# A two-layer trunk on one core: another order in the mixer and the last head, and a third tile's products ahead of the first down products of each SwiGLU

## The chip, the cores and the metric

The kernel runs on one core of one Trainium2 chip. The metric is the device time of one execution in microseconds (us). Engines are named as in the profile: PE is TensorE, DVE VectorE, ACT ScalarE, POOL GpSimd, SP the engine that issues most loads.

## The reference

What must be computed, cut to the two layers (T = 1024 frames, D = 1024 features, float32 in and out):

```python
def conv_pool_mixer(h, w_in, dw_w, dw_b, ln_g, ln_b, pool_w, pool_scale, w_out):
    z = h @ w_in
    a = a_val * jax.nn.sigmoid(a_gate)
    a = depthwise_causal_conv(a, dw_w, width=31) + dw_b
    a = jax.nn.silu(layernorm(a, ln_g, ln_b))
    d = trailing_mean(u, window=2/4/8/16 per group) - u
    p = einsum('btgc,gcd->btgd', d, pool_w) * pool_scale
    return jnp.concatenate([a, p], axis=-1) @ w_out
def hgrn2_mixer(h, w_in, lb, gn_g, w_out):
    q, f_raw, i, g = jnp.split(h @ w_in, 4, axis=-1)
    f = lb + (1 - lb) * sigmoid(f_raw); k = 1 - f
    o = chunkwise_recurrence(q, k, i, f)
    o = head_rmsnorm(o) * gn_g * jax.nn.silu(g)
    return o @ w_out
def swiglu_ffn(h, w1, w3, w2):
    return (jax.nn.silu(h @ w1) * (h @ w3)) @ w2
```

Layer 0 adds the mixer of the normalized h to h, then the SwiGLU of the normalized h; layer 1 does so with HGRN; a last RMSNorm follows.

## The kernel before

Frames lie along the free axis of a tile, features along the partitions. The 1024 frames are two halves of 512 (`half`); a tile is 128 features by 512 frames, and 8 of them (`KT`) make a half of the residual. The residual lives in HBM, in `hd[k]`. A step either adds to it by an accumulating DMA from POOL's queue (`accumulate`, L304), or fetches it, adds a PE bank to it on DVE (`add_residual`, L328) and puts it back. `Ahead` (L315) fetches three tiles before they are needed.

Each float32 product is made of three matmuls of a rounded high part and a low rest (`gemm_steps`, L154): high by high, high by low, low by high, 512 columns each. So each operand is split, high part on ACT, low part on DVE (`split` L170 for activations, `load` L135 for weights: SP fetches 128x1024 float32 into one of two raw buffers, ACT and DVE write a pair out of three). PE banks come from two pools of four (`gbank`, `mbank`).

The order on each engine is fixed when the program is built: a scheduler takes the instructions by priority, which is the order of the code unless a block raises it (`tc.high_priority`, `sooner`). Each engine and each DMA queue then works its list in order, waiting at the head of the list.

**Mixer** (`layer0_mixer`, L335). x is transposed on PE, normalized and split; `project_a` makes the gated conv input of four channel tiles; `conv` (L464) runs the 31 taps of channel tiles 0, 1 and 2 on DVE in steps of 512 columns; tile 3 goes through PE (`conv_by_phase`, L512) with weights that `conv_blocks` builds on POOL from the taps (L506), and its result is regrouped by small DMAs into `cb` and brought into y3 by four activations (L539). The pooling groups follow (`project_u`, `map_u`, `mean_u`: banks u, uw and um; the tile v between them, L583, is made by ACT). Then the projection of the pooled half (banks op, 16 of them, 12 products each), with ACT copying each bank out and POOL adding it to the residual; the layer norm of the conv half (L621 on: ysum, mu, lss, the broadcast bc_ln), both halves of the frames one after the other; and the conv half's projection (banks oa), which fetches the residual, adds and puts back. All of the pooling steps and the op products stand in one block of raised priority, the layer norm in one of still higher priority.

**SwiGLU** (`ffn`, L668). 22 hidden tiles in blocks of 2, 4, 4, 4, 4, 4 (`BLOCKS`, L664). A tile's two products over all 1024 frames are seven products of half the depth (`Up.p1` to `p7`, 12 matmuls each) with sums of weights (`sums`) and sums of inputs (b11, b21, b22, t1 to t4); `gate` applies the norm's row and the SiLU. The first pair of tiles goes step by step together (p1, p2, p6, p7, p4, then gate(0), p5, p3, gate(1)). Behind each block come its down products (banks f0o and f1o); for the first block these are 16 banks of 6 products.

**HGRN** (`hgrn`, L883). 8 heads. `recur` (L974) runs one head's recurrence for one half; at each of its steps it yields a number (`BEFORE`, L911) of filler products which the caller pulls in front of the step (`advance`). The filler of a head is the projection of the next head (pf, pq, the values pv, and pg, the output gate) and, where `OUT_AT` (L912) says so, products of the output projection (banks ho) of heads that are done. What is left of the filler follows at the head's end. The output projection of the filler is accumulated; for that ACT copies the bank into one of three buffers (`temp`). The last two steps behind head 7 fetch the residual, add and put back (h_ho).

```python
BEFORE = {0: 7, 2: 4, 4: 5, 6: 3, "k": 2, "S": 2, "o": 1, "T": 10}
OUT_AT = {3: (([0, 1], (0, 1)),), 7: (([2, 3], (0, 1)), ([4, 5], (0,)))}
```

## Time and profile before

| | us |
|---|---|
| median of 3 runs (lowest, highest) | 2321.64 (2317.51, 2322.33) |
| profiled execution, its own time | 2319.05 |
| its span in the profile | 2317.2 |
| PE busy | 2233.5 (96%) |
| DVE busy | 1566.5 (68%) |
| ACT busy | 836.7 (36%) |
| POOL busy | 330.1 (14%) |

The mean granted clock of PE over the span is 0.983 of full speed. The mixer runs from the start to about 325 us, the first SwiGLU to about 1000, HGRN to about 1625, the second SwiGLU and the last norm to the end. The profile's rows are of one execution; a wait's time is put down to the event that came last. In the stretches below, the first figure behind the length is PE's busy time, so length minus that is its idle time.

### The profile page before, as it was taken

The numbers are of one execution on the slowest core, as the hardware profiler recorded it, in microseconds if no ns is written. First come the engines' busy times: TensorE is split into PE (matmuls) and PEld (weight loads), VectorE is DVE, ScalarE is ACT, GpSimd is POOL, SyncE is SP. The second block draws the span as 40 slices with busy tenths as digits, with TensorE's granted clock in tenths as the row PEclk, the third lists the DMA queues.
The fourth block names the chain that finished last, engine by engine and source line by source line (L and its number), as shares of the span: only waits on it lengthen the run. The fifth ranks groups of instructions, "written<-read, shape, count | busy, mean of one in ns | idle before, by whom it ended". The sixth has DMA issues, their size and how long they took to land.

```text
span 2317.2 us, 28669 instructions
## 1 busy us (share of the span) xinstructions
PE 2233.5 (96%) x10814; PEld 1873.9 (81%) x10814; DVE 1566.5 (68%) x2924; ACT 836.7 (36%) x1354; POOL 330.1 (14%) x341
## 2 busy tenths in 40 slices
PE   7998999999999999999999899988899999999998
PEld 6887777888888888888888789876688888888877
DVE  6999695738373736858887387866956464737377
ACT  5223654333333333532222322234543333323336
POOL 1030334010101010310000200035220101010110
PEclk9998999999999999999999999998999999999999
DMA  7103735161515252631111611176153434242544
GB/s 230 56 11 80 186 116 109 55 127 55 117 54 113 62 111 71 210 100 37 46 46 37 118 37 47 37 140 188 55 109 91 91 86 96 74 99 73 100 136 155
DMA packets 220746, 218.18 MB, mean 94 GB/s; under 512 B 9332, under 2 KB 181568, under 8 KB 220608
## 3 DMA queue, kind: packets, MB, share of 16 engines
q1 hardware_dynamic: 186320, 130.18, 18.5%
q0 software_dynamic: 27008, 73.41, 17.1%
q10 hardware_dynamic: 7280, 12.76, 1.5%
q8 instruction: 85, 1.39, 0.2%
q14 instruction: 53, 0.43, 0.1%
HBM read 137.67 MB, written 77.59 MB: 93 GB/s over the span
## 4 chain that ended last, share of the span: by engine, by line
PE 56%; issue 25%; DVE 9%; POOL 2%; DMA 2%; ACT 1%; SPq 0%; ACTq 0%; POOLq 0%; DVEq 0%
PE f1o L160 3%; PE f1o L161 3%; PE f1o L162 3%; PE f0o L161 3%; PE f0o L162 3%; PE f0o L160 3%; DVE y L470 3%; POOL hd L308 1%; DVE wl L143 1%; PE op L160 1%; PE op L161 1%; PE op L162 1%; PE f_5p L735 1%; PE f_18p L735 1%; PE f_18p L733 1%
## 5 line engine op out<-in xcount | busy, mean ns | idle before, releaser
L143 DVE TENSOR_TENSOR wl<-wr,wh 128x1024 fp32r<-128x1024 f32 x130 | 161.4, 1241 | 108.4 <-ACT wh L142 107.7
L142 ACT CAST wh<-wr 128x1024 fp32r<-128x1024 f32 x132 | 138.5, 1051 | 147.1 <-PE pg L161 19.3
L470 DVE SCALAR_TENSOR_TENSOR y<-a,dww,y 128x512 f32<-128x512 f32 x180 | 137.1, 810 | 0.4
L308 POOL DMA_DIRECT2D hd<-ev_ho x40 | 34.8, 892 | 542.0 <-ACT ev_ho L307 534.4
L1029 DVE COPY_PREDICATED S<-masks,pl 128x128 f32<-128x128 uint8 x288 | 92.2, 341 | 13.2 <-PE pl L1011 12.0
L160 PE MATMUL f1o<-f1g_1h,wh 128*128 128x512 f32 (+1 forms) x208 | 74.6, 359 | 1.9 <-ACT f1ev L858 1.9
L1011 PE MATMUL pl<-M,K 128*128 128x192 f32 x384 | 73.0, 334 | 3.5 <-DVE M L998 3.5
L161 PE MATMUL f1o<-f1g_1l,wh 128*128 128x512 f32 (+1 forms) x208 | 74.1, 356 | 0.0
L162 PE MATMUL f1o<-f1g_1h,wl 128*128 128x512 f32 (+1 forms) x208 | 74.1, 356 | 0.0
L160 PE MATMUL f1o<-f1g_0h,wh 128*128 128x512 f32 x176 | 69.3, 393 | 4.2 <-DVE f_0u L762 2.9
L160 PE MATMUL f0o<-f0g_0h,wh 128*128 128x512 f32 x176 | 69.2, 393 | 2.4 <-DVE f_0u L762 2.4
L1011 PEld LDWEIGHTS pl<-M,K 128*128 128x128 f32 x384 | 65.5, 194 | 6.9 <-ACT M L1001 2.2
L161 PE MATMUL f1o<-f1g_0l,wh 128*128 128x512 f32 x176 | 69.5, 395 | 1.1 <-DVE f1g_0l L174 1.1
L160 PE MATMUL f0o<-f0g_1h,wh 128*128 128x512 f32 x176 | 68.6, 390 | 1.4 <-ACT f0ev L858 1.4
L162 PE MATMUL f1o<-f1g_0h,wl 128*128 128x512 f32 x176 | 69.1, 392 | 0.4 <-DVE wl L143 0.4
L162 PE MATMUL f0o<-f0g_0h,wl 128*128 128x512 f32 x176 | 69.2, 393 | 0.0
L161 PE MATMUL f0o<-f0g_0l,wh 128*128 128x512 f32 x176 | 69.1, 393 | 0.0
L161 PE MATMUL f0o<-f0g_1l,wh 128*128 128x512 f32 x176 | 68.6, 390 | 0.1
L162 PE MATMUL f0o<-f0g_1h,wl 128*128 128x512 f32 x176 | 68.5, 389 | 0.0
L864 ACT COPY f1ev<-f1o 128x512 f32<-128x512 f32 x64 | 37.4, 585 | 80.1 <-PE f1o L162 66.1
L864 ACT COPY f0ev<-f0o 128x512 f32<-128x512 f32 x64 | 37.4, 585 | 78.7 <-PE f0o L162 67.2
L866 POOL DMA_DIRECT2D hd<-f0ev x32 | 27.8, 869 | 219.6 <-ACT f0ev L864 217.3
(5437 smaller groups left out, 7075.6 us busy)
## 6 DMA issues: line engine op xcount, KB each, us to landing
wr<-in_ffn_w SPq DMA_DIRECT2D x56, 512.0 KB, 3.4
...
hd<-ev_ho POOLq DMA_DIRECT2D x40, 256.0 KB, 5.2
h_f<-hd POOLq DMA_DIRECT2D x32, 256.0 KB, 5.4
...
```

Of the source, the lines that this page charges most:

```text
L142: nc.scalar.copy(wh, raw)
L143: (leng or nc.vector).tensor_tensor(wl, raw, f32(wh), ALU.subtract)
L160: nc.tensor.matmul(ps, lh, xh, start=k == 0, stop=False)
L161: nc.tensor.matmul(ps, lh, xl, start=False, stop=False)
L162: mm = nc.tensor.matmul(ps, ll, xh, start=False, stop=k == len(xs) - 1)
L308: nc.gpsimd.dma_start(out=hd[k][:, half(hf)], in_=o, accum_op=ALU.add)
L470: nc.vector.scalar_tensor_tensor(acc, tap(at, j, t0, n), dww[:, j, c:c + 1], acc, ALU.mult, ALU.add)
L735: mm = nc.tensor.matmul(ps, wl[:, k], xh, start=False, stop=k == len(xs) - 1)
L864: nc.scalar.copy(os[i][:, half(hf)], product(mg, i, hf, w))
L866: nc.gpsimd.dma_start(out=hd[mg + i], in_=os[i], accum_op=ALU.add)
L1011: nc.tensor.matmul(pl[:, c], K[:, ch[cc]], M[:, :, cc * 64:(cc + 1) * 64], start=True, stop=True)
L1029: nc.vector.copy_predicated(sv, mk.unsqueeze(1).to_broadcast([P, 2, 64 // w, w]), pl[:, :, j, :].rearrange("p c (b n) -> p c b n", n=w))
```

## The change

In the mixer: x is fetched by column halves, and the first half's squares and the second weight split come behind the first casts (`fetch_weights`, `split_weights`, `last_cast`). The conv of channel tile 0 does 8 taps in halves and the other 23 over all 1024 columns, that of tile 1 all 31 so. The PE conv's weights come ready from HBM through `load`. The activations that write y3 stand behind the pooling steps. The layer norm and the pooled projection become two functions; the order of the code is layer norm of half 0, pooled projection, four residual fetches on SP's queue, layer norm of half 1. In the SwiGLU stage the broadcast's multiplications for the row of both halves go to POOL, and tile 2 does p1 and p2 in front of the first down products. In HGRN the output gate's products go from the projection of the next head into the head's own filler; half of the first two heads' output products move from head 3 to head 4, and half to head 7; the last head has its own numbers of filler steps, and its accumulates use staged buffers.

```diff
-    def load(src, shape, leng=None):
+    def fetch_weights(src, shape):
         uid[0] += 1
-        i, n = uid[0], shape[0] * shape[1]
-        raw = wpool.tile([P, 1024], F32, tag="wraw", name=f"wr{i}", bufs=NRAW)[:, :n]
+        raw = wpool.tile([P, 1024], F32, tag="wraw", name=f"wr{uid[0]}", bufs=NRAW)[:, :shape[0] * shape[1]]
+        nc.sync.dma_start(out=raw.rearrange("p (a b) -> p a b", a=shape[0]), in_=src)
+        return raw, shape, uid[0]
+
+    def split_weights(raw, shape, i, leng=None):
+        n = shape[0] * shape[1]
...
-        nc.sync.dma_start(out=raw.rearrange("p (a b) -> p a b", a=shape[0]), in_=src)
...
+    def load(src, shape, leng=None):
+        return split_weights(*fetch_weights(src, shape), leng)
...
-    def broadcast(y, name, room, bank=mbank):
+    def broadcast(y, name, room, bank=mbank, eng=nc.vector):
...
+            eng.tensor_tensor(dg.rearrange("p (t q) -> p t q", q=P), ident.unsqueeze(1).to_broadcast([P, 4, P]),
...
+            ps = broadcast(y, f"{self.name}{hf}", staged, bank, eng)
...
-    def accumulate(k, hf, ps, name):
-
-        o = temp(f"ev_{name}{k}_{hf}")
+    def accumulate(k, hf, ps, name, room=temp):
+
+        o = room(f"ev_{name}{k}_{hf}")
         nc.scalar.copy(o, ps)
...
-    def fetch(k, hf, name):
+    def fetch(k, hf, name, eng=nc.gpsimd):
...
+        eng.dma_start(out=h, in_=hd[k][:, half(hf)])
...
-                xt = []
-                for t in range(4):
-                    xt.append([staged(f"x{hf}_{t}_{i}") for i in range(2)])
-                    for i in range(2):
+                xt = [[None] * 2 for _ in range(4)]
+                for i in range(2):
+                    for t in range(4):
+                        xt[t][i] = staged(f"x{hf}_{t}_{i}")
                         nc.sync.dma_start(out=xt[t][i], in_=a["x"][0, hf * H + t * P:hf * H + (t + 1) * P, i * H:(i + 1) * H])
                 return xt
...
-                v0 = squares(0, x0)
                 pend = [(0, k, transpose_in(0, x0, k, gbank if 3 < k < 7 else mbank)) for k in range(KT)]
-                wg = load(*cols(w_in, 4), leng=nc.gpsimd)
-                x1 = load_x(1)
+                wr, x1 = fetch_weights(*cols(w_in, 4)), load_x(1)
                 for p in pend[:7]:
                     keep(*p)
-                hold(*pend[0])
+                with tc.issue_after(last_cast[0]):
+                    hold(*pend[0])
                 keep(*pend[7])
                 for p in pend[1:]:
                     hold(*p)
+                with tc.issue_after(last_cast[0]):
+                    wg = split_weights(*wr, leng=nc.gpsimd)
+                    v0 = squares(0, x0)
                 for k in range(KT):
...
-            ybuf = [[staged(f"y{c}_{hf}") for hf in range(NH)] for c in range(NC4)]
-            for y in sum(ybuf[:NC4 - 1], []):
+            ywide = [pool.tile([P, T], F32, name=f"y{c}", bufs=1) for c in range(2)]
+            ybuf = [[y[:, half(hf)] for hf in range(NH)] for y in ywide]
+            ybuf += [[staged(f"y{c}_{hf}") for hf in range(NH)] for c in range(2, NC4)]
+            for y in ywide + ybuf[2]:
...
-            def conv(c, hf):
-                acc, at, t0, n = ybuf[c][hf], ats[c], hf * H, H
-                for j in range(CW):
+            def conv(c, hf=None, taps=range(CW)):
+
+                at = ats[c]
+                acc, t0, n = (ywide[c], 0, T) if hf is None else (ybuf[c][hf], hf * H, H)
+                for j in taps:
...
-            traw = pool.tile([P, PH * PS * PH], F32, name="traw", bufs=1)
-            nc.sync.dma_start(out=traw, in_=a["conv_taps"])
-            taps = [pool.tile([P, PH * PS * PH], F32, name=f"taps{z}", bufs=1) for z in "hl"]
-            nc.scalar.copy(taps[0].bitcast(F32R), traw)
-            nc.vector.tensor_tensor(taps[1], traw, taps[0], ALU.subtract)
...
-                uid[0] += 1
-                w = []
-                for t, z in zip(taps, "hl"):
-                    m = wpool.tile([P, 1024], F32R, tag=f"w{z}", name=f"cw{z}{i}", bufs=NSPLIT)[:, :n * P]
-                    nc.gpsimd.tensor_tensor(
-                        m.rearrange("p (a b) -> p a b", b=PG), diag.unsqueeze(1).to_broadcast([P, n * PH, PG]),
-                        t[:, i * PH:(i + n) * PH].unsqueeze(2).to_broadcast([P, n * PH, PG]), ALU.mult)
-                    w.append(m.rearrange("p (a b) -> p a b", b=P))
-                return w
+                return load(a["conv_taps"][:, i * P:(i + n) * P].rearrange("p (a b) -> p a b", b=P), (n, P))
...
+                yield
                 for i in range(2):
                     for hf in range(NH):
                         yv = ybuf[c][hf].rearrange("p (t r) -> p r t", r=PH)
                         bv = bp[i].rearrange("p (r t) -> p r t", r=2)[:, :, hf * PT // 2:(hf + 1) * PT // 2]
                         nc.scalar.activation(yv[:, 2 * i:2 * i + 2, :], bv, AF.Identity,
                                              bias=prm[:, R_DWB + c:R_DWB + c + 1])
-                yield
...
             for hf in range(NH):
-                conv(0, hf)
+                conv(0, hf, range(8))
+            conv(0, taps=range(8, CW))
             project_a(1)
-            for hf in range(NH):
-                conv(1, hf)
+            conv(1)
             project_a(NC4 - 1)
 
...
-                for m2 in range(4):
-                    wo = load(*cols(w_out, 2 * m2, 2, 4, 4))
-                    for mo in range(2):
-                        for hf in range(NH):
-                            po = gbank(f"op{m2}_{mo}_{hf}")
-                            gemm(po, wo, mo, ps_[hf])
-                            accumulate(2 * m2 + mo, hf, po, "op")
+                for _ in cbp:
+                    pass
 
             as_ = [[None] * NC4 for _ in range(NH)]
-            for hf in range(NH):
+
+            def layer_norm(hf):
                 ysum = staged(f"ysum{hf}")
...
-                        t = staged(f"ly{hf}_{c}")
-                        nc.vector.tensor_tensor(t, ybuf[c][hf], bc, ALU.mult)
+                        t = ybuf[c][hf]
+                        nc.vector.tensor_tensor(t, t, bc, ALU.mult)
                         nc.scalar.activation(t, t, AF.Silu, scale=prm[:, R_LNG + c:R_LNG + c + 1],
                                              bias=prm[:, R_LNB + c:R_LNB + c + 1])
                         as_[hf][c] = split(t, f"a{c}_{hf}")
+
+            def pooled_out(steps):
+                with tc.high_priority(offset=HI):
...
+            layer_norm(0)
+            pooled_out(range(4))
             ahead = Ahead("oa", [(k, hf) for hf in range(NH) for k in range(KT)])
+            with tc.high_priority(offset=HI):
+                for k in range(4):
+                    ahead.got[k, 0] = fetch(k, 0, "oa", nc.sync)
+            layer_norm(1)
             for hf in range(NH):
...
-                    rs[hf] = norm.rows(hf, ys[hf], gbank)
+                    rs[hf] = norm.rows(hf, ys[hf], gbank, nc.gpsimd)
...
+
+        with sooner():
+            third = Up(2)
+        third.p1()
+        third.p2()
         j0 = 0
         pending = iter(())
         for b, nb in enumerate(BLOCKS):
             for j in range(j0, j0 + nb) if b else ():
-                x = Up(j)
+                x = third if j == 2 else Up(j)
                 for _ in x.sums():
                     pass
-                for p in (Up.p1, Up.p2, Up.p6, Up.p7, Up.p4):
+                for p in (Up.p6,) if j == 2 else (Up.p1, Up.p2, Up.p6):
+                    p(x)
+                for p in (Up.p7, Up.p4):
...
-        OUT_AT = {3: (([0, 1], (0, 1)),), 7: (([2, 3], (0, 1)), ([4, 5], (0,)))}
+        OUT_AT = {4: (([0, 1], (0,)),), 7: (([0, 1], (1,)), ([2, 3], (0, 1)), ([4, 5], (0,)))}
+        BEFORE_LAST = {0: 8, 2: 5, 4: 6, 6: 5, "k": 5, "S": 4, "o": 3, "T": 10}
...
+
+        def output_gate(hd, G):
             w = load(*cols(w_in, 24 + hd))
             for hf in range(NH):
...
-        def recur(hd, hf, late, F, Q, K, G):
-            nm = f"{hd}_{hf}"
+        def recur(hd, hf, late, G, F, Q, K):
+            nm, before_step = f"{hd}_{hf}", BEFORE if hd + 1 < HEADS else BEFORE_LAST
...
-                yield BEFORE[lv]
+                yield before_step[lv]
...
-                            accumulate(mg + mo, hf, po, f"ho{hds[0]}_")
+                            accumulate(mg + mo, hf, po, f"ho{hds[0]}_", staged if late else temp)
...
-        def filler(hd, tiles):
+            return [[None] * NH for _ in range(3)]
+
+        def filler(hd, tiles, G):
+            yield from output_gate(hd, G)
             if hd + 1 < HEADS:
                 yield from project(hd + 1, tiles)
             for hds, halves in OUT_AT.get(hd, ()):
-                yield from project_out(hds, halves)
+                yield from project_out(hds, halves, late=hd + 1 == HEADS)
...
-                    m[r, :, :, k, o] = w[CW - 1 - lag].reshape(PH, PG).T
-    return m.reshape(P, PH * PS * PH)
+                    for q in range(PH):
+                        m[r, c, q, k, o, c] = w[CW - 1 - lag, q * PG + c]
+    return m.reshape(P, PH * PS * P)
```

What moves, at three places, as the two kernels' lists have it.

ACT's list near the end of the pooling steps, before (cy2 is the conv's last PE bank copied out; y3_0, y3_1 are the two halves of channel tile 3; v3 is pooling group 3):

```order
L528 COPY cy2_1486<-cp2_1485 128x512
L539 ACTIVATE y3_0_562<-cb0_1299,prm_84 128x2x128
L539 ACTIVATE y3_1_563<-cb0_1299,prm_84 128x2x128
L583 ACTIVATE v3_1_1674<-uw3_1_1669,y_x1_450 128x128
L539 ACTIVATE y3_0_562<-cb1_1300,prm_84 128x2x128
L539 ACTIVATE y3_1_563<-cb1_1300,prm_84 128x2x128
L583 ACTIVATE v3_1_1674<-uw3_1_1669,y_x1_450 128x128 x3
L176 ACTIVATE p3_0h_1687<-um3_0_1679,prm_84 128x512
L176 ACTIVATE p3_1h_1700<-um3_1_1691,prm_84 128x512
```

and now:

```order
L524 COPY cy2_1426<-cp2_1425 128x512
L579 ACTIVATE v3_1_1614<-uw3_1_1609,y_x1_450 128x128 x4
L182 ACTIVATE p3_0h_1627<-um3_0_1619,prm_84 128x512
L182 ACTIVATE p3_1h_1640<-um3_1_1631,prm_84 128x512
L313 COPY ev_op0_0_1773<-op0_0_0_1760 128x512
L536 ACTIVATE y3_0_562<-cb0_1233,prm_84 128x2x128
L536 ACTIVATE y3_1_563<-cb0_1233,prm_84 128x2x128
L536 ACTIVATE y3_0_562<-cb1_1234,prm_84 128x2x128
L313 COPY ev_op0_1_1789<-op0_0_1_1776 128x512
L536 ACTIVATE y3_1_563<-cb1_1234,prm_84 128x2x128
```

The four activations on y3 stood between cy2 and the rest of v3; they now stand behind v3, p3 and the first copy of an op bank.

PE's list in the last head, from the transposes of its keys (pk7_0) to the state products (pS7_0), before (ho banks are the filler, og the gated outputs of earlier heads):

```order
L1050 MATMUL pk7_0_12689<-ident_75,K7_0_12175 128x128 x4
L160 MATMUL ho2_4_1_0_12685<-og3_0h_10197,wh99_12650 128x512
L161 MATMUL ho2_4_1_0_12685<-og3_0l_10198,wh99_12650 128x512
L162 MATMUL ho2_4_1_0_12685<-og3_0h_10197,wl99_12651 128x512
L160 MATMUL ho2_4_1_1_12702<-og2_1h_9837,wh99_12650 128x512
L161 MATMUL ho2_4_1_1_12702<-og2_1l_9838,wh99_12650 128x512
L162 MATMUL ho2_4_1_1_12702<-og2_1h_9837,wl99_12651 128x512
L1057 MATMUL pS7_0_12706<-V7_0_11563,KT7_0_12694 128x128 x4
```

and now:

```order
L167 MATMUL ho0_4_2_1_12501<-og1_1l_9076,wh99_12477 128x512
L168 MATMUL ho0_4_2_1_12501<-og1_1h_9075,wl99_12478 128x512
L166 MATMUL ho0_4_3_1_12518<-og0_1h_8488,wh99_12477 128x512
L167 MATMUL ho0_4_3_1_12518<-og0_1l_8489,wh99_12477 128x512
L168 MATMUL ho0_4_3_1_12518<-og0_1h_8488,wl99_12478 128x512
L166 MATMUL ho0_4_3_1_12518<-og1_1h_9075,wh99_12477 128x512
L167 MATMUL ho0_4_3_1_12518<-og1_1l_9076,wh99_12477 128x512
L168 MATMUL ho0_4_3_1_12518<-og1_1h_9075,wl99_12478 128x512
L166 MATMUL ho2_0_0_0_12534<-og2_0h_9505,wh100_12530 128x512
L167 MATMUL ho2_0_0_0_12534<-og2_0l_9506,wh100_12530 128x512
L168 MATMUL ho2_0_0_0_12534<-og2_0h_9505,wl100_12531 128x512
L1076 MATMUL pS7_0_12538<-V7_0_11529,KT7_0_12510 128x128 x4
```

pk7_0 stands two rows ahead of this second piece: there are now 12 filler products between the two steps where there were 6, and they belong to the second half of heads 0 and 1 and to heads 2 and 3.

PE's list at the first down product of the first SwiGLU stage, before (p3 of tile 1, then the down bank f0o):

```order
L734 MATMUL f0_1p3_3069<-hn_nf0b22_3l_2968,f0_1s4h_2851 128x512
L735 MATMUL f0_1p3_3069<-hn_nf0b22_3h_2967,f0_1s4l_2852 128x512
L160 MATMUL f0o0_0_0_0_0_3098<-f0g0_0h_3005,wh30_3092 128x512
L161 MATMUL f0o0_0_0_0_0_3098<-f0g0_0l_3006,wh30_3092 128x512
L162 MATMUL f0o0_0_0_0_0_3098<-f0g0_0h_3005,wl30_3093 128x512
```

and now:

```order
L743 MATMUL f0_2p2_3049<-hn_nf0b21_3l_2355,f0_2a1h_3029 128x512
L744 MATMUL f0_2p2_3049<-hn_nf0b21_3h_2354,f0_2a1l_3030 128x512
L166 MATMUL f0o0_0_0_0_0_3070<-f0g0_0h_2941,wh30_3065 128x512
L167 MATMUL f0o0_0_0_0_0_3070<-f0g0_0l_2942,wh30_3065 128x512
L168 MATMUL f0o0_0_0_0_0_3070<-f0g0_0h_2941,wl30_3066 128x512
```

The 12 products of p1 and the 12 of p2 of tile 2 stand between p3 of tile 1 and the first down bank. In SP's list the transfer of tile 2's first weights now stands in front of the two transfers of down weights, where it stood behind them.

## Rows read from the trace of the kernel before

**Rows 1.** The page: busy time, share of the span, instructions of each engine.
```profile
PE 2233.5 (96%) x10814; PEld 1873.9 (81%) x10814; DVE 1566.5 (68%) x2924; ACT 836.7 (36%) x1354; POOL 330.1 (14%) x341
```

**Rows 2.** Stretches: start:end, length, busy us (instructions) per engine, granted clock, DMA share, GB/s.
```profile
150.00:200.00 50.00, 47.12 (x297) 42.02 (x295) 50.00 (x66) 16.74 (x35) 11.02 (x6) 0.97 0.09 28
200.00:250.00 50.00, 43.07 (x181) 35.47 (x182) 39.35 (x67) 24.02 (x39) 11.04 (x13) 0.86 0.62 130
250.00:300.00 50.00, 45.10 (x191) 36.29 (x190) 38.54 (x58) 27.79 (x42) 21.07 (x25) 0.93 0.71 203
350.00:400.00 50.00, 46.16 (x190) 36.69 (x189) 28.50 (x37) 23.94 (x38) 22.23 (x21) 0.95 0.63 123
1000.00:1300.00 300.00, 300.00 (x1790) 265.52 (x1789) 218.72 (x634) 88.58 (x176) 6.02 (x7) 1.00 0.18 50
1300.00:1325.00 25.00, 18.86 (x103) 15.90 (x101) 7.58 (x17) 7.97 (x15) 7.88 (x10) 0.93 0.89 153
1525.00:1550.00 25.00, 21.73 (x108) 18.07 (x106) 13.85 (x43) 7.32 (x16) 6.09 (x7) 0.93 0.66 120
1550.00:1575.00 25.00, 19.02 (x94) 15.18 (x94) 12.71 (x37) 9.70 (x16) 8.58 (x12) 0.93 0.86 171
1650.00:1675.00 25.00, 20.71 (x77) 15.27 (x76) 23.99 (x37) 11.12 (x17) 8.53 (x5) 0.91 0.14 42
1675.00:1700.00 25.00, 23.11 (x100) 18.77 (x99) 9.35 (x12) 13.18 (x22) 14.69 (x17) 0.98 0.76 126
```

**Rows 3.** What PE waited for: total us, times, longest us.
```profile
PE ho L160 <- DVE h_ho L329: 9.9, 4, 5.0
PE um L593 <- ACT v L583: 7.5, 2, 7.3
PE ho L160 <- ACT ev_ho L307: 6.4, 5, 2.6
...
PE pS L1057 <- ACT KT L1052: 4.7, 2, 2.7
PE oa L160 <- DVE h_oa L329: 4.6, 1, 4.6
PE av L161 <- DVE hn_0l L177: 3.9, 2, 3.6
...
PE f1o L160 <- DVE f_0u L762: 2.9, 1, 2.9
PE f0o L160 <- DVE f_0u L762: 2.4, 1, 2.4
PE u L162 <- DVE wl L143: 2.3, 1, 2.3
```

**Rows 4.** Timeline of PE: start us, duration us, two neighbouring products of 512 columns.
```profile
361.19 0.39 PE L734 MATMUL f_1p<-hn_nf0b_3l,f_1s4h 128*128 128x512 f32 x1
361.42 0.39 PE L735 MATMUL f_1p<-hn_nf0b_3h,f_1s4l 128*128 128x512 f32 x1
```

**Rows 5.** Timeline of ACT near 205 us, in brackets the idle time before and its end.
```profile
205.25 1.25 ACT L539 ACTIVATE y<-cb,prm 128x256 f32<-128x256 f32 x2 [6.20 <-DMA cb<-cy]
```

**Rows 6.** The page, DMA issues: count, size of each, median us to landing.
```profile
hd<-ev_ho POOLq DMA_DIRECT2D x40, 256.0 KB, 5.2
```

**Rows 7.** Timeline of DVE from 163 us, steps of the conv.
```profile
163.69 1.40 DVE L470 SCALAR_TENSOR_TENSOR y<-a,dww,y 128x512 f32<-128x512 f32 x2
...
165.68 5.38 DVE L470 SCALAR_TENSOR_TENSOR y<-a,dww,y 128x512 f32<-128x512 f32 x4
```

**Rows 8.** Timeline of POOL at the same time, building the conv's weights.
```profile
166.82 2.36 POOL L506 TENSOR_TENSOR cwl<-diag,tapsl 128x1024 fp32r<-128x1024 f32 x1
```

**Rows 9.** Groups of DVE instructions: count, busy us, mean ns, idle before and releasers.
```profile
L143 DVE TENSOR_TENSOR wl<-wr,wh 128x1024 fp32r<-128x1024 f32 x130 | 161.4, 1241 | 108.4 <-ACT wh L142 107.7
...
L972 DVE TENSOR_TENSOR G<-G,sg 128x512 f32<-128x512 f32 x16 | 11.0, 689 | 6.3 <-ACT sg L971 6.3
```

**Rows 10.** Timeline of ACT near 1528 us.
```profile
1527.83 0.59 ACT L1052 COPY KT<-pk 128x512 f32<-128x512 f32 x1 [2.71 <-DMA hd<-ev_ho]
```

55 lines of the change are left out of this document (28 added, 27 removed).

## Prediction

> **What bounds the kernel now.** I read the page first. TensorE (PE) is busy 96% of the span and VectorE (DVE) 68% [rows 1]: the floor is PE's own work, and nothing in the diff takes a product away from PE. What can be won is the time in which PE stands idle or runs at its lower clock. The table by stretches says where that is. From 1000 to 1300 us PE has 300.00 us of work in 300.00 us at a granted clock of 1.00 [rows 2]: there is nothing to win. The stretches from 150 to 400 us (mixer and start of the first SwiGLU), at 1300, at 1525 to 1575 and at 1650 to 1700 have idle time, and a clock below 1.00 beside it [rows 2]. The clock has two levels here, 1.2 and 2.4 GHz, so a mean of 0.86 over 50 us is up to 7 us of full-speed work lost (0.14 x 50); less, where PE was idle anyhow. The lower level shows only in stretches that hold idle time, so a wait that goes should take its clock loss with it. Third, the list of what PE waits for [rows 3] names the producer of each idle piece. These are the terms below. A 512-column product starts 0.23 us after the one before it [rows 4].
>
> **The change, part by part.** All against the profiled execution, 2319.05 us; the median of the three runs is 2.6 us above that.
>
> *Start.* PE waits 3.6 us in one piece for the low half of the first normalized tile [rows 3]. The order after has the eight low halves first on DVE and moves squares and a weight split behind the first cast; x comes in by column halves, so the first tile's transposes need four transfers where they needed seven. Between nothing and -3.6; I take **-3**, since nothing else in that chain changes.
>
> *Mixer: the conv's drain.* ScalarE (ACT) stood 6.20 us before the first activation that writes y3, waiting for the small transfers that regroup the conv's result [rows 5]; the activations of v, which PE needs, were queued behind it, and PE waited 7.3 us [rows 3]. The clock of that stretch is 0.86, 7 us of loss, of which at most half the wait was idle anyhow: 3.7 us more. In the order shown, the y3 activations stand behind p3 and the first op copy, so no PE step waits for them directly: -11. But now the layer norm's sum, on DVE in order, needs y3, and its first PE step (mu) comes behind it. If all of ACT's 6.2 us returned there with a clock loss like before it would cost 8; PE's order has mu 29 op products, 6.7 us, further back, so I charge 3 (0 to 8). Net **-8** (-3 to -11).
>
> *Mixer: the second layer norm.* PE waits 4.6 us for banks that the residual add on DVE empties [rows 3]; in order, that add stood behind the second layer norm's work. The change puts the norm's code for the second half behind the pooled products and the first four residual fetches. The stretch holds 4.9 us idle and 3.5 of clock (0.07 x 50) [rows 2]. Between nothing, if DVE, which is then the late engine, has only moved its work, and -8.1. I take **-6**.
>
> SP's queue now holds the first four residual fetches between the third and the fourth weight load of this projection. Each waits for the accumulate of its tile, the 1st to 7th of 16 banks of 12 products, and the load behind them is needed 9 banks and 72 products later, 180 x 0.23 = 41 us; hidden, unless an accumulate needs over 30 us for its 5.2 [rows 6].
>
> *Mixer: the taps and the wide conv.* GpSimd (POOL) built the conv's weights, 2.36 us for 1024 columns, and beside it four DVE steps of the conv took 5.38 us where two took 1.40 a moment before [rows 7, 8]. So 1.35 us instead of 0.70 each; over ten such POOL steps (eight of 1024 columns, two of 512), some 20 us, DVE loses about half. PE waits 2.3 us for a weight split just there [rows 3], and the stretch's clock of 0.97 is 1.5 us. Now the weights come by DMA and cost DVE five splits, 4 x 1.24 and a half one, 5.6 us [rows 9]. Against that, 53 pairs of conv steps become steps of 1024 columns; by the rows of two-operand steps a pair saves 2 x 0.689 - 1.241 = 0.14 us [rows 9], 7 us in all (nothing, if a wide step costs twice a narrow one). DVE is thus 1 us shorter in work and some 9 us shorter in time. On PE that is worth the wait and its clock, -3.8, at best; I take **-3** (0 to -3.8). The extra 2.4 MB of transfers lie where the DMA engines are busy 9% [rows 2].
>
> *Rows of the second SwiGLU operand on POOL.* Four multiplications a stage move from DVE (0.69 us [rows 9]) to POOL (half of 2.36, about 1.2 us [rows 8]); two of them in a row stand before a PE step. **+1** for both stages (0 to +2). The Trainium skill speaks against this part: "GPSIMD Engine Reference", section 8, says that GpSimd shares its SBUF interfaces with VectorE and contends with two-input VectorE steps; the rows agree (1.35 us against 0.70 [rows 7]). By that rule, an estimate from those rows, four DVE steps beside POOL's would take 2.6 us longer a stage, and the sum would be 2278 if PE waited for all of them.
>
> *Third tile before the first down products.* In the first stage PE waits 2.4 us for the gate of the pair [rows 3]; the stretch has 3.84 us idle and 2.5 of clock (0.05 x 50) [rows 2]. 24 products that need none of it now stand there: 24 x 0.23 = 5.5 us, which covers either wait. Their weight transfer goes to SP's queue ahead of the two down weights, and the second of those waits for a raw buffer: landing within 5.2 us, if it takes as long as an accumulate [rows 6], and two splits of at most 1.24 [rows 9], 7.7 in all, against 5.5 + 24 x 0.23 = 11 us of PE work in front of its first use. So it is hidden; without that cover it would cost those 7.7. **-5** (-2.4 to -6.3). In the second stage the wait is 2.9, the idle time 4.29 and 1.89, the clock 2.25 and 0.5: 8.9 in all [rows 2, 3]; **-7** (-2.9 to -8.9).
>
> *HGRN, head 3.* PE waits 6.4 us for copies out of the output projection's banks [rows 3], most of it at 1300, where 6.14 us are idle and 1.75 are clock [rows 2]. The cause is room: a copy's buffer is free when its accumulate has landed, 5.2 us later [rows 6], and there are three, while a bank fills every 6 products, 1.4 us. The change spreads half of these products behind the query products of head 5 in the filler of head 4, and half into head 7. **-5.5** (-2 to -7.9).
>
> *HGRN, head 7.* Its filler had 33 us of projection for 16 steps; with its own gate (48 products, 10.9 us) and the second half of heads 0 and 1 (as much) it has 55, and the counts of the last head put more of it in front of each step: 6 more products before pS in the order shown. The copies go to staged rooms instead of the three. Before: KT waits for DMA 2.71 us on ACT [rows 10], so pS waits 4.7 in all [rows 3]; with the rest, 3.27 + 5.98 us idle and 2 x 1.75 of clock, 12.75 [rows 2]. **-9** (-4 to -12.75).
>
> *Output projection behind it.* PE waits 9.9 us for the residual's add, 5.0 in the longest [rows 3]: the first fetch can only go when the last accumulate has landed. Fewer accumulates stand in front of it now, but the last still comes late. **-3** (0 to -5).
>
> Sum: -3 - 8 - 6 - 3 + 1 - 5 - 7 - 5.5 - 9 - 3 = -48.5, so 2319.05 - 48.5 = 2270.5 for the profiled execution and 2.6 more for a median: **2273**. With every term at its smaller bound it is -12 (about 2310), at its larger -67 (about 2255).
>
> **The rivals.** *1. The mixer's wait only moves.* DVE is busy 50.00 of 50 us before 200 and is the engine behind mu and the second norm. If the sum of the first norm still comes late by ACT's 6.2 us, and the norm's work then stands in front of the residual adds, the drain gives -3, the second norm 0: 2273 + 5 + 6 = 2284. For it: DVE's full stretch. Against: 9 us less of DVE time ahead of the sum.
>
> *2. Transfers, not rooms, bound head 7.* With more rooms more accumulates are in flight at once; the DMA engines are 0.66 and 0.86 busy there [rows 2]. Then each lands later, the first residual fetch with them, and the 9 + 3 of the last two terms shrink to nothing: 2285. The Trainium skill, "DMA: Bandwidth & Descriptors", section "Issuing engines are not separate DMA queues", says that transfers from any engine share the same 16 DMA engines, so that a fetch moved from POOL's queue to SP's gains nothing in bandwidth either. No row here shows the two queues against each other. For rival 2: the busy shares. Against: ACT waited while the rooms, not the engines, were full.
>
> *3. Slower: the heads' boundaries.* The output gate's 48 products stood at the end of a head's filler, between the query's products and the next head's first step (pd), which needs the query. Now the query's last 24 products, 5.5 us, are all that lies between for heads 1, 3 and 7 and less cover than before for the others. DVE must do the query's scaling (0.69 us [rows 9]) behind the last head's norm. From about 5 us of backlog on DVE on, PE waits at each of seven boundaries; at 12 us of backlog that is 7 x (7 + 1.7 of clock, as at 1300) = 61 us, more than all gains: 2334. Against it: DVE is busy 218.72 of 300 us there and PE waits for nothing [rows 2].
>
> *4. It does not do what it says*, since the scheduler, not the code, sets the order. The three pieces of the order shown exclude this for their places.
>
> **How the numbers follow.** A measurement of this kernel can tell 0.2%, 4.6 us, from no change. Chances: the forecast 0.63; rival 1 0.18; rival 2 0.13; rival 3 0.04, of which 0.01 falls within 0.2%; the rest, 0.02, is gains below 4.6 us that no single rival describes. Faster 0.94, same 0.03, slower 0.03. The range: both of the first rivals at once give 2273 + 23 = 2296, the largest gains 2255 + 2.6; with all at one bound unlikely, I take 2254 to 2296.
>
> **What would show it.** Right: the table of stretches has under 3 us idle from 200 to 250 and at 1300 to 1325, clock 0.95 or more; no wait of um for v; no wait of the first down products for f_0u; KT without a DMA in front; pS without a wait. Wrong: a wait of mu for ysum above 4 us, or of oa for the residual add as long as before (rival 1); ho waiting for h_ho over 10 us (rival 2); pd waiting for Q in each head (rival 3). An idle piece in the heads from 400 to 1000 would mean that the raw buffers' rotation is disturbed beyond the stage's start, which I priced at nothing.

## The result and the profile after

Before: 2319.57 us, the median of all its runs beside these; after: **2291.93 us**, the median of four (2289.44 to 2295.67). The ratio is 0.9884 [0.9861, 0.9906]: 28 us faster, where the forecast of 2273 stood 47 below the same median. The time lies inside the range, near its upper end, so some terms came and some did not. The profiled execution took 2289.44 us, its span is 2287.7 us.

The first thing to read is the table of stretches of the kernel after, cut at the first product of each stage (the op-oa stage at the first op product behind the last um product; start:end, length, busy us and instructions of PE, PEld, DVE, ACT, POOL, granted clock, DMA share, GB/s). A wait in front of a stage's first product counts to the stage before it.

```profile
0.00:94.80 94.80, 82.62 (x359) 65.07 (x360) 73.99 (x124) 38.86 (x76) 7.16 (x18) 0.96 0.48 155
94.80:195.60 100.80, 100.80 (x591) 89.14 (x589) 97.36 (x112) 34.08 (x68) 0.12 (x1) 1.00 0.23 67
195.60:295.20 99.60, 91.47 (x401) 73.04 (x401) 80.78 (x128) 53.07 (x82) 35.59 (x38) 0.99 0.72 179
295.20:351.70 56.50, 48.76 (x188) 36.98 (x189) 51.02 (x87) 28.50 (x44) 17.50 (x12) 0.90 0.13 43
351.70:433.80 82.10, 79.65 (x348) 65.27 (x349) 46.36 (x68) 29.87 (x45) 22.14 (x22) 1.00 0.48 103
...
1464.10:1536.70 72.60, 72.60 (x382) 61.96 (x380) 46.45 (x134) 33.32 (x60) 26.61 (x31) 1.00 0.78 151
1536.70:1585.40 48.70, 36.59 (x147) 28.19 (x146) 33.93 (x38) 22.06 (x34) 24.43 (x27) 0.93 0.76 228
1585.40:1640.20 54.80, 46.56 (x188) 35.51 (x188) 52.50 (x88) 28.79 (x44) 16.56 (x13) 0.94 0.15 51
```

The same view of the kernel before, for its conv with the pooling, for the first pair of tiles, and for head 7:

```profile
96.00:210.50 114.50, 104.69 (x590) 91.68 (x589) 113.93 (x152) 31.79 (x67) 21.39 (x11) 0.95 0.14 43
...
310.20:364.20 54.00, 46.25 (x189) 35.57 (x188) 52.19 (x92) 29.62 (x46) 11.99 (x9) 0.94 0.17 55
...
1504.00:1572.90 68.90, 59.67 (x304) 49.77 (x302) 42.70 (x129) 26.31 (x49) 20.39 (x24) 0.95 0.75 137
```

Conv and pooling take 100.80 us where they took 114.50, and PE is busy in all of them at clock 1.00. In head 7 PE is busy 72.60 of 72.60 us; before it was busy 59.67 of 68.90 (the stage is longer because 78 more instructions of PE were put into it). The pair did not get shorter but longer, 56.50 against 54.00.

The table below gives the length of every stage in us for all kernels of this study, from the start times of PE's timeline. "op-oa" is the output projections of the mixer with both norms, "third" the third tile (its names begin with f_2, since tiles count from 0) with the first down products and the tiles of f_3 and f_4, "out" HGRN's output projection behind head 7; 0 and 1 are the two SwiGLU stages. Stages in which two kernels do not differ still scatter by up to 3 us; pair and third stage together, in the kernels where they are as in after (u_mixer, u_drain, u_head, h_rooms, h_counts), are 137.9 to 141.5 and 138.0 to 141.4 us.

```
           start  conv op-oa  pair0 third0 rest0 head0-6 head7   out pair1 third1 rest1   span
before      96.0 114.6  99.6   54.0   82.7 541.4   515.6  68.9  44.3  53.6   83.9 562.5 2317.2
after       94.8 100.8  99.7   56.5   82.1 542.1   488.1  72.6  48.7  54.8   83.6 563.8 2287.7
u_mixer     96.0 114.6  99.1   55.3   84.0 542.3   488.1  72.6  49.4  55.5   82.5 563.5 2302.9
u_drain     95.3 109.0  92.9   55.4   82.5 542.2   487.9  72.6  48.2  55.1   84.2 564.0 2289.3
u_head      95.8 100.8 101.8   57.3   83.4 541.4   513.9  68.7  41.9  56.3   85.1 562.6 2308.9
h_rooms     94.3 100.8 100.5   56.4   82.1 542.0   487.8  93.6  49.7  56.0   85.1 563.6 2311.9
h_counts    95.1 100.8  99.2   56.3   85.2 541.3   489.1  57.8  65.9  56.0   84.5 563.5 2294.6
u_third     93.7 100.8 100.7   54.4   84.1 541.3   488.1  72.6  47.3  55.5   82.8 563.2 2284.5
f_mbank     94.9 100.8  99.4   53.8   87.5 541.3   489.3  72.6  47.5  51.9   87.5 563.4 2290.1
f_half      94.7 100.8 100.3   56.2   79.0 541.3   487.9  72.6  49.4  54.9   80.6 562.2 2279.9
f_su        93.6 100.8 101.1   54.8   80.4 541.3   487.4  72.6  49.8  52.1   81.3 563.2 2278.3
a_deep      96.2 100.8  97.8   56.7   84.9 542.1   487.2  72.6  43.3  59.7   83.8 564.1 2289.3
combo2      93.4 100.8  97.5   53.6   84.3 541.3   488.6  72.6  49.3  56.0   83.9 563.8 2285.3
f_su_best   94.3 100.8  99.0   51.1   80.5 541.3   486.4  72.6  49.8  52.9   81.4 562.6 2272.8
```

From before to after: start -1.2, conv to op-oa -13.7, HGRN with its projection -19.4, the two pair and third stages together +2.8, the rest +2.0. That is the whole of the 29.5 us between the spans. The heads and the conv delivered; the third tile did not.

What PE waits for after (total us, times, longest us):

```profile
PE ho L166 <- DVE h_ho L335: 8.2, 5, 5.0
PE f_0p L742 <- ACT hn_nf0t_1h L179: 7.0, 2, 6.3
...
PE f_2p L742 <- DVE f_0u L771: 5.6, 2, 3.3
PE f_3p L744 <- DVE f_3a1l L713: 4.4, 2, 2.2
PE f_0p L742 <- DVE h_ho L335: 4.0, 1, 4.0
PE av L167 <- DVE hn_1l L183: 2.8, 6, 0.8
PE bc_nf L208 <- POOL dg_nf L206: 2.8, 2, 1.7
...
PE mu L621 <- DVE ysum L620: 0.7, 1, 0.7
```

Against [rows 3]: um's wait for v (7.5), ho's for ev_ho (6.4), pS's for KT (4.7), oa's 4.6 and u's 2.3 are gone or below 1 us. The down products' waits for f_0u (2.4 and 2.9) are gone too, but three new names stand in their place: f_0p, f_2p and f_3p, the first products of a SwiGLU stage, of its third tile and of its fourth. The four rows of these names shown above are 21 us in all.

### The profile page after: what moved, and what is told of

It is laid out like the page before. It is cut to its first block, busy times and chain, and to the rows that moved or that the text cites. A ratio compares the mean times of both kernels' runs of the same rounds, so it can differ in the third digit from the quotient of the medians.

```text
span 2287.7 us, 28586 instructions
## 1 busy us (share of the span) xinstructions
PE 2222.2 (97%) x10814; PEld 1864.5 (82%) x10814; DVE 1552.7 (68%) x2865; ACT 840.4 (37%) x1360; POOL 313.8 (14%) x333
## 3 DMA queue, kind: packets, MB, share of 16 engines
q0 software_dynamic: 26688, 72.37, 17.5%
## 4 chain that ended last, share of the span: by engine, by line
PE 56%; issue 25%; DVE 9%; DMA 4%; POOL 3%; ACT 2%; ACTq 0%; POOLq 0%; DVEq 0%; SPq 0%
PE f0o L167 3%; PE f0o L166 3%; PE f0o L168 3%; PE f1o L166 3%; PE f1o L167 3%; PE f1o L168 3%; POOL hd L314 1%; DMA f_3w<-in_ffn_w 1%; PE u L166 1%; PE u L168 1%; PE u L167 1%; PE ag L166 1%; PE f_5p L744 1%; PE ag L167 1%; PE ag L168 1%
## 5 line engine op out<-in xcount | busy, mean ns | idle before, releaser
L146 DVE TENSOR_TENSOR wl<-wr,wh 128x1024 fp32r<-128x1024 f32 x137 | 167.7, 1224 | 104.2 <-ACT wh L145 103.7
L145 ACT CAST wh<-wr 128x1024 fp32r<-128x1024 f32 x139 | 145.3, 1047 | 211.8 <-PE pv L934 28.3
L483 DVE SCALAR_TENSOR_TENSOR y<-a,dww,y 128x512 f32<-128x512 f32 (+1 forms) x127 | 118.3, 972 | 0.7
```

The source lines that it names most:

```text
L145: nc.scalar.copy(wh, raw)
L146: (leng or nc.vector).tensor_tensor(wl, raw, f32(wh), ALU.subtract)
L483: nc.vector.scalar_tensor_tensor(acc, tap(at, j, t0, n), dww[:, j, c:c + 1], acc, ALU.mult, ALU.add)
```

## The experiments

All times are medians with their ratio to the kernel before, which was run again beside each group of kernels (its medians there: 2318.43 to 2320.23). The kernel after was not, so a difference of 2 to 3 us against it says little. Each diff is against the kernel after.

**Part by part.** First each of the three largest parts was undone by itself; the rows on POOL were not.

*u_mixer*: the mixer as before, all else as after.

```diff
...
+                    m = wpool.tile([P, 1024], F32R, tag=f"w{z}", name=f"cw{z}{i}", bufs=NSPLIT)[:, :n * P]
+                    nc.gpsimd.tensor_tensor(
...
+                conv(0, hf)
...
-            layer_norm(0)
-            pooled_out(range(4))
...
```

> The changed kernel with the whole mixer as before, its start too. By the trace the mixer's own stretches gained 21.1 us (0.9 to 96 us, 13.7 to the last um, 6.5 in op and oa) and the pair of tiles behind it lost 8.9. Theory A: the loss belongs to the mixer (residual fetches and adds that come late because PE arrives earlier): undone, the time rises by 12.2 only, to 2304, and the pair's first product waits under 2 us again. Theory B: the loss belongs to another part (the rows on POOL, the third tile's early weight load): undone, the time rises by 21, to 2313.

Measured: 2307.37 us, 0.9963 [0.995, 0.9976], 15.4 above after. Conv is 114.6 us again, op-oa and pair 0 are 0.6 and 1.2 shorter: the part is worth 15 us, nearly all in the conv's stage. The wait of 6.3 us in front of the first pair is gone, and the oa banks wait 4.0 us for the residual add again.

*u_head*: HGRN as before (no staged rooms, its old filler and counts).

```diff
-        OUT_AT = {4: (([0, 1], (0,)),), 7: (([0, 1], (1,)), ([2, 3], (0, 1)), ([4, 5], (0,)))}
-        BEFORE_LAST = {0: 8, 2: 5, 4: 6, 6: 5, "k": 5, "S": 4, "o": 3, "T": 10}
+        OUT_AT = {3: (([0, 1], (0, 1)),), 7: (([2, 3], (0, 1)), ([4, 5], (0,)))}
...
-                            accumulate(mg + mo, hf, po, f"ho{hds[0]}_", staged if late else temp)
+                            accumulate(mg + mo, hf, po, f"ho{hds[0]}_")
```

> The changed kernel with HGRN as before: output gate in the next head's projection, output products at head 3 and 7, counts and rooms of before. By the trace the part is worth 5.9 in head 3, 13.9 in head 7 and 3.8 in the output projection, 23.6 in sum: 2315.5. If the head's stretches were only shortened by what comes before them (a DMA burst that moved), it would be worth less than 12.

Measured: 2309.56 us, 0.9968 [0.9956, 0.998], 17.6 above after; heads and projection together 624.5 us against 609.4. The waits of ho for ev_ho (5.6) and of pS for KT (5.2) are back.

*u_third*: the third tile's products p1 and p2 stand behind the first down products again.

```diff
-        with sooner():
-            third = Up(2)
-        third.p1()
-        third.p2()
...
-                x = third if j == 2 else Up(j)
+                x = Up(j)
...
```

> The changed kernel with the third tile's p1 and p2 back behind the first down products of each SwiGLU stage. Theory A (as predicted): the 24 products cover the wait for the pair's gate, 5 us in the first stage and 7 in the second, so taking them away costs about 12: 2304. Theory B: the wait only moves. In the changed kernel's trace the third tile's first product waits 2.4 and 3.3 us for a bank that DVE has not emptied, and the fourth tile's p1 waits 2.2 each time for its weights, whose transfers land late behind the 16 accumulates of the first down products. By B the time stays within 2 us of 2292, the waits of f0o and f1o for f_0u (2.4 and 2.9) come back, and the waits of f_2p and f_3p go.

Measured: 2286.46 us, 0.9878 [0.9857, 0.9899]. Pair and third stage together are 138.5 and 138.3 us; after has 138.6 and 138.4. So this part of the change brings **nothing**, where the forecast had 12 us. (The median without it is 5.5 us below after, but the intervals of the two ratios overlap nearly whole, and no stage shows the difference.) The waits only changed names: without it the down products wait for f_0u 2.4, for the gate 4.2 and for evicted banks 2.7 and 1.2; with it f_2p and f_3p wait 10.0.

**Head 7: rooms or transfers?**

A room is a buffer that holds a copied bank until its accumulate has landed. *h_rooms*: the last head's copies go through the three old buffers; its filler and its counts stay as changed.

```diff
-                            accumulate(mg + mo, hf, po, f"ho{hds[0]}_", staged if late else temp)
+                            accumulate(mg + mo, hf, po, f"ho{hds[0]}_", temp)
```

> The changed kernel with the last head's accumulates copied into the three small buffers again instead of staged tiles; counts of filler unchanged. Theory A (rooms bound head 7): the waits of ACT for landed accumulates come back, and with them pS for KT and ho for ev_ho, 8 to 12 us: 2300 to 2304. Theory B (more filler per step was enough): the waits on PE stay below 2 us in head 7 and the time within 3 us of 2292.

Measured: 2311.82 us, 0.9974 [0.9963, 0.9985]; head 7 grows from 72.6 to 93.6 us. In this kernel's list of waits (first ACT, then PE; total, times, longest) the copies wait for a room and PE for the copies:

```profile
ACT ev_ho L313 <- DMA hd<-ev_ho: 35.3, 19, 5.9
```

```profile
PE ho L166 <- DVE h_ho L335: 10.7, 4, 5.7
PE ho L166 <- ACT ev_ho L313: 9.9, 8, 5.4
...
PE pS L1076 <- ACT KT L1071: 5.5, 2, 2.9
```

One line costs 20 us, more than undoing the whole HGRN part: with more filler in the head, the old three rooms would have been worse than before. The rooms are the bound, not the transfers: after moves more through head 7 (DMA share 0.78 against 0.75) and PE does not wait.

*h_counts*: the other half, the old counts of filler per step in the last head.

```diff
-        BEFORE_LAST = {0: 8, 2: 5, 4: 6, 6: 5, "k": 5, "S": 4, "o": 3, "T": 10}
+        BEFORE_LAST = BEFORE
```

> The changed kernel with the last head's numbers of filler steps as in the other heads; rooms stay staged. If the numbers matter, pS waits for KT and pl for M again in head 7, each 1 to 3 us, 4 to 8 in sum: 2296 to 2300, and the filler that is left over stands at the head's end. If the rooms alone did it, head 7 stays without waits and the time within 3 us of 2292.

Measured: 2295.94 us, 0.9902 [0.9887, 0.9916], 4 above after. Head 7 stays without a wait at 57.8 us; what is not placed there runs behind it, and the projection takes 65.9 instead of 48.7. Together they are 2.4 us longer, and ho's wait for h_ho grows from 8.2 to 13.1: the last accumulates come later, and the first fetch of the residual with them. The seven kernels with this head and projection as in after take 119.9 to 122.4 us for the two, so 123.7 lies just outside. By the medians the counts are worth some 4 us; 2.4 of them are seen here.

**The third tile: why nothing?**

*f_mbank*: p1 of the third tile takes its bank from the other pool, so that it does not wait for f_0u's step on DVE.

```diff
-        third.p1()
+        third.p1(mbank)
```

> The changed kernel with the third tile's p1 in a bank of the other pool, which is free earlier. Theory A (the third tile's products wait for a bank only): the waits of 2.4 and 3.3 us before f_2p go, and 4 to 7 us with them: 2285 to 2288. Theory B (the next bound is the burst of accumulates behind the first down products, which start with them): the waits of f_2p go, those of f_3p for its weights stay at 2 us or grow, and the gain is under 5.

Measured: 2292.34 us, 0.9885 [0.987, 0.9899]. f_2p waits no more; pair 0 is 53.8 instead of 56.5, and pair 1 51.9 instead of 54.8. All of it and more comes back in the next stage, 87.5 against 82.1 and 83.6, where f_3p now waits 7.6 us in all. So f_3p, the fourth tile's first product, is the second limit. In the kernel after, the view of its raw weight tile f_3w (line, engine, operation, start from issue to issue; then its landing) says:

```profile
L703 SPq DMA_DIRECT2D f_3w<-in_ffn_w x2: 368/368/368, 370.5 to 380.4; - x2
...
DMA to landing us min/median/max: 10.5/13.8/17.1
```

f_2w, of the same 512 KB, lands after 3.8 us; the two loads of f_3w take 17.1 and 10.5. From 370 to 390 us the DMA engines are full, with these loads and the 16 accumulates of the first down block, which are issued from 361.8 to 380.4 us (DMA view of the kernel after, 355 to 400 us: size and median us to landing, then stretches as above):

```profile
hd<-f0ev POOLq DMA_DIRECT2D x16, 256.0 KB, 7.8
f_3w<-in_ffn_w SPq DMA_DIRECT2D x2, 512.0 KB, 13.8
f_2w<-in_ffn_w SPq DMA_DIRECT2D x1, 512.0 KB, 3.8
```

```profile
370.00:380.00 10.00, 10.00 (x46) 8.29 (x45) 0.78 (x2) 4.87 (x9) 6.89 (x8) 1.00 1.10 199
380.00:390.00 10.00, 10.00 (x46) 8.29 (x45) 1.04 (x2) 1.17 (x2) 0.87 (x1) 1.00 1.09 218
```

*f_half*: leaves out half of those accumulates, so its result lacks their sums and only its times count.

```diff
-                                nc.gpsimd.dma_start(out=hd[mg + i][:, half(hf)], in_=o, accum_op=ALU.add)
+                                if hf == 0:
+                                    nc.gpsimd.dma_start(out=hd[mg + i][:, half(hf)], in_=o, accum_op=ALU.add)
```

> The changed kernel without the accumulates of the second half of the frames behind the first block's down products in both SwiGLU stages (those 8 transfers of 16 are left out, so the second half lacks this block's share). Theory A (the 16 transfers delay tile 3's weights): its two weight loads land in 4 to 6 us instead of 10.5 and 17.1, and f_3p no longer waits for f_3a1l: 4.4 us less on PE, both stages together. Theory B (the two raw buffers are the bound): the loads are issued as late as now, and f_3p still waits about 2 us in each stage.

Measured in one run: 2281.68 us. f_3w is issued at the same times, and lands as f_2w does:

```profile
L703 SPq DMA_DIRECT2D f_3w<-in_ffn_w x2: 368/368/368, 370.7 to 380.7; - x2
...
DMA to landing us min/median/max: 3.7/4.0/4.4
```

f_3p's waits are gone, and the third stages are 3.1 and 3.0 us shorter; pair and third stage together, 135.2 and 135.5 us, lie below all kernels that have them as in after. So it was the burst of accumulates that delayed the load, and not its issue or a buffer. The Trainium skill, "DMA: Bandwidth & Descriptors", section "Issuing engines are not separate DMA queues", says that transfers from all engines end up on the same 16 DMA engines; this pair of runs agrees (POOL's accumulates, SP's load: 17.1 us against 4.4).

*f_su*: both limits taken away at once, with nothing left out. p1 takes the other pool's bank, and the third tile's first raw weights get a buffer of their own, so that the fourth tile's loads need not wait for it and go out ahead of most of the burst.

```diff
-            third = Up(2)
-        third.p1()
+            third = Up(2, raw=lambda n: wide(n) if n.endswith("w1") else wpool.tile([P, 1024], F32, tag="wraw", name=n, bufs=NRAW))
+        third.p1(mbank)
```

> The changed kernel with the third tile's p1 in the other bank pool and its first raw weights in a free wide buffer, so that both raw buffers stay with the rotation and the fourth tile's first load goes out ahead of the burst of accumulates. Theory A (burst and late issue delay tile 4's weights, index 3): f_3w's first load lands within 5 us, f_2p and f_3p wait under 1 us each, and the third tile's products at last give what was forecast, some 8 to 11 us less than the changed kernel: 2281 to 2284. Theory B (its second load still lands late in the burst and DVE's sum of it stands in front of the split that PE needs): f_3p still waits 2 to 4 us, gain under 4.

Measured: **2282.17 us, 0.9838 [0.982, 0.9856]**, 9.8 below after. The loads now go at 355.5 and 370.4 us:

```profile
L703 SPq DMA_DIRECT2D f_3w<-in_ffn_w x2: 367/368/368, 355.5 to 370.4; - x2
...
DMA to landing us min/median/max: 4.1/8.4/12.6
```

f_2p and f_3p wait no more; pair and third stage are 135.2 and 133.4 us together, where after has 138.6 and 138.4. The second load still lands in 12.6 us, but it now has the time. So the third tile's place gains only together with both edits. The extra raw buffer without the third tile's early products was not run; how much of the gain it would bring alone stays open.

**The mixer: what is its limit?**

*u_drain*: the activations that write y3 stand between the conv's phases and the last pooling again.

```diff
-                yield
                for i in range(2):
...
+                yield
...
-                for _ in cbp:
-                    pass
```

> The changed kernel with the activations that write y3 back between the conv's last phases and the last pooling steps. By the prediction's largest term: ACT waits 6 us for the regrouping transfers again, PE waits 7 us for v, and with the clock the time rises by 8 to 11: 2300 to 2303. If what is gained there only comes back at mu, mu's wait of 0.7 us falls to nothing and the time stays within 3 us of 2292.

Measured: 2291.54 us, 0.9886 [0.9868, 0.9904]: no difference. The old wait is back in full on ACT (in this kernel's timeline), and PE's um waits 5.58 us for v behind it, at 199.99 us:

```profile
198.56 1.27 ACT L535 ACTIVATE y<-cb,prm 128x256 f32<-128x256 f32 x2 [5.05 <-DMA cb<-cy]
199.62 0.32 ACT L579 ACTIVATE v<-uw,y_x 128x128 f32<-128x128 f32 x1
```

Conv is 109.0 us instead of 100.8, but op-oa is 92.9 instead of 99.7: the third tile starts at 352.6 instead of 351.7 us. PE comes 8 us later to a place at which it would have waited. In the kernel after, that place is the first f_0p (PE's timeline, idle time in brackets):

```profile
288.58 0.39 PE L168 MATMUL oa<-a_1h,wl 128*128 128x512 f32 x1
295.23 0.77 PE L742 MATMUL f_0p<-hn_nf0b_0h,f_0a1h 128*128 128x512 f32 x1 [6.26 <-ACT hn_nf0t_1h L179]
```

The wait is put down to ACT; but f_0p writes a bank that a residual add on DVE empties, that add ends just before 295.2 too, and in u_drain and a_deep the same wait is put down to it (timeline of DVE, then of POOL):

```profile
285.45 1.76 DVE L726 TENSOR_TENSOR f_0w<-f_0w 128x512 f32<-128x512 f32 x1 [3.99 <-POOL f_0s L725]
...
294.40 1.28 DVE L335 TENSOR_TENSOR h_oa<-h_oa,oa 128x512 f32<-128x512 f32 x2
```

```profile
284.13 1.29 POOL L725 TENSOR_TENSOR f_0s<-f_0w,f_0w 128x512 f32<-128x512 f32 x1 [2.35 <-issue]
285.37 2.99 POOL L230 TENSOR_TENSOR nacc_nf<-nacc_nf,sq_nf 128x512 f32<-128x512 f32 x2
288.30 1.64 POOL L318 DMA_DIRECT2D h_oa<-hd  x3
```

Three residuals are fetched from POOL's queue at 288.30, behind POOL's squares and the weight sum f_0s; DVE does the add at 294.40, behind the first tile's weight sums, for which it had itself stood 3.99 us waiting for POOL's f_0s.

*a_deep*: the residual is fetched five ahead instead of three, in the mixer's and in HGRN's projection.

```diff
-            for kk in self.order[:i + 3]:
+            for kk in self.order[:i + self.depth]:
...
+            ahead = Ahead("oa", [(k, hf) for hf in range(NH) for k in range(KT)], 5)
```

> The changed kernel with residual tiles fetched five ahead instead of three, in the mixer's conv-half projection and in the HGRN output projection. Theory A (the pair of tiles waits for an oa or ho bank because the residual add on DVE comes late, behind a fetch that POOL issued late): f_0p's waits of 6.3 and 4.0 us at the start of both SwiGLU stages fall below 2 each, and the time falls by 4 to 9, to 2283 to 2288. Theory B (DVE's own work at that point is the bound): the adds come earlier, the input splits later, the waits turn up at the second or third product group instead, and the time stays within 2 us of 2292.

Measured: 2290.33 us, 0.9875 [0.9858, 0.9891], 1.6 below after, which the scatter covers. f_0p's wait falls from 6.3 to 3.5 and is now named for DVE's h_oa, but what op-oa and out gain (1.9 and 5.4 us) pair and third stages lose (third 0 2.8, pair 1 4.9). Fetching earlier helps the fetch; the sum gains nothing clear of the scatter.

**Two combinations.** *combo2*: u_third with a_deep, and the rows of the second operand back on DVE; *f_su_best*: f_su with the same two.

```diff
-                    rs[hf] = norm.rows(hf, ys[hf], gbank, nc.gpsimd)
+                    rs[hf] = norm.rows(hf, ys[hf], gbank)
```

> The changed kernel without the third tile's early products, rows on DVE, fetches five ahead. If the third tile is worth nothing as it stands: 2282 to 2286. If the three act against each other, 2290 or more.

> As the kernel before, with the rows' multiplications back on DVE and residual fetches five ahead. If the gains add up: 1.5 from the rows (bc_nf waits of 2.8 in all for POOL), 1.5 to 3 from the fetches, so 2277 to 2282. If DVE at the start of the stage is the bound, the same time as that kernel within 2 us.

Measured: combo2 2284.32 us, 0.9849 [0.9827, 0.9871]; **f_su_best 2276.49 us, 0.9813 [0.9796, 0.983]**, faster than both kernels of this case, 15.4 below after. Against f_su it gains 2.1 us in op-oa and 3.7 in pair 0, where both edits act; combo2 minus u_third, the same two edits without f_su, is -2.1, which the scatter covers. What each of the two is worth alone beside f_su was not run. What PE waits for in f_su_best:

```profile
PE ho L166 <- DVE h_ho L335: 12.5, 2, 7.5
PE pt_prm L87 <- DMA prow<-in_params: 6.4, 1, 6.4
PE f_0p L742 <- DVE h_oa L335: 3.5, 1, 3.5
```

The output projection's 12.5 us, in two pieces, is now the largest entry.

## Why the prediction was right and wrong

**Right: direction, HGRN, and most of the named waits.** The range held. Heads 3 and 7 with the output projection were forecast at -17.5; undoing them costs 17.6, and the stages are 19.4 us shorter. Rooms were the mechanism: h_rooms gives back 20 us with one line. Rival 2 (transfers instead of rooms) fell with it, and rival 3 never showed: heads 0 to 6 lost time nowhere. The inner split was off, since head 7 gave more than its 9 and the projection nothing (its longest wait is 5.0, as in [rows 3]); I priced the two separately though the second begins where the first one's last accumulate lands.

**Wrong: the third tile, -12 forecast, 0 measured.** The step that failed is "24 products that need none of it now stand there ... which covers either wait". They need one thing of it: a PSUM bank which the pair's own f_0u step on DVE frees ([rows 3] name f_0u; I read it as the gate). Here is DVE at that point in the kernel after:

```profile
344.93 2.00 DVE L713 TENSOR_TENSOR f_2a1l<-f_2w,f_2a1h 128x1024 fp32r<-128x1024 f32 x1
346.85 1.78 DVE L784 TENSOR_TENSOR f_0c<-f_0c,f_0c 128x512 f32<-128x512 f32 x1
...
350.89 0.68 DVE L771 TENSOR_TENSOR f_0u<-f_0u,f_0p 128x512 f32<-128x512 f32 x1
```

and in the kernel before:

```profile
357.42 2.00 DVE L143 TENSOR_TENSOR wl<-wr,wh 128x1024 fp32r<-128x1024 f32 x1
359.35 1.77 DVE L775 TENSOR_TENSOR f_0c<-f_0c,f_0c 128x512 f32<-128x512 f32 x1
...
363.38 0.67 DVE L762 TENSOR_TENSOR f_0u<-f_0u,f_0p 128x512 f32<-128x512 f32 x1
```

DVE's list is as long as it was: the third tile's split stands where the split of the first down weights stood, and f_0u begins 5.96 us behind it in both. The first product behind the pair needs that bank either way, and waits 2.4 us either way; f_mbank, which takes another bank, ends the wait. The second miss is in "So it is hidden". I followed the third tile's own load and found it in time, which it was (3.8 us). I did not follow the next one: moving 24 products ahead of the down block takes them away from behind it, where they had covered the fourth tile's load. In u_third its two loads go out at 378.9 and 383.6 us, behind the last of the accumulates, and the second is there at 387.6; in after they go out at 370.5 and 380.4, amid them, and the second is there at 390.9. My sign for such trouble, idle time from 400 us on by a disturbed rotation of the raw buffers, looked too late (f_3p waits at 393 us) and for another cause. f_su shows the price: 3.4 and 5.0 us of pair and third stage against after, of which f_half alone gives 3.4 and 2.9.

**Wrong in its reason: the mixer, -17 forecast for three terms, -13.7 measured.** The drain's -8 is 0 by u_drain, though its wait went as forecast and mu waits 0.7 as hoped. What the traces show instead is DVE's time. The conv's steps in the whole kernel (groups of DVE's instructions: count, busy us, mean ns, idle time before), before and after:

```profile
L470 DVE SCALAR_TENSOR_TENSOR y<-a,dww,y 128x512 f32<-128x512 f32 x180 | 137.1, 810 | 0.4
```

```profile
L483 DVE SCALAR_TENSOR_TENSOR y<-a,dww,y 128x512 f32<-128x512 f32 (+1 forms) x127 | 118.3, 972 | 0.7
```

The same work costs DVE 19 us less; in the conv's stage five more weight splits take back 4.9. Part of the 16.6 us by which DVE's busy time in the conv's stage falls comes back in op-oa (75.1 us before, 80.8 after). I had worked out "some 9 us shorter in time" for DVE and then valued it at 3, because PE waited for a split only 2.3 us. But the pair's first product follows DVE's last conv step, not PE's waits. That step and the first f_0p, before and after (timelines of DVE and PE; f_0p after is the row at 295.23 above):

```profile
229.11 0.75 DVE L470 SCALAR_TENSOR_TENSOR y<-a,dww,y 128x512 f32<-128x512 f32 x1
310.19 0.39 PE L733 MATMUL f_0p<-hn_nf0b_0h,f_0a1h 128*128 128x512 f32 x1
```

```profile
218.44 0.75 DVE L483 SCALAR_TENSOR_TENSOR y<-a,dww,y 128x512 f32<-128x512 f32 x1
```

From the end of that step to f_0p it is 80.3 and 79.9 us with the old mixer (before, u_mixer), 75.6 to 77.5 with the new one, in u_drain 76.0, and 72.5 to 73.7 with residuals fetched five ahead. So a wait of PE's that lies ahead of f_0p, as v's, costs nothing while DVE's chain is the later one: rival 1 came true, not at mu, but at the start of the pair. By the same rows f_0p comes 15.0 us earlier because DVE's first conv step starts 3.5 earlier, the conv ends 7.1 sooner after it, and 4.3 go between its end and f_0p, where the second norm's place (-6) acts. This is read from traces: no run undid the wide conv, the ready weights or the second norm's place alone, so what each brings by itself stays open.

**The rest.** Start: -1.2 instead of -3 at PE's first u product. Rows on POOL, +1: PE's wait for dg_nf is 2.8 after and 1.9 before, and 2.5 in f_su_best, with the rows on DVE; the size was not measured alone. The sum fell short by 19.0 us of span (29.5 for 48.5): 13.8 in the pair and third stages (+2.8 where third tile and rows were to give -11), 3.3 in the mixer, 1.8 at the start, 2.0 in the rest, less 1.9 that HGRN gave more.
